# Five edits to a hybrid convolution, retention and expert layer: retention heads grouped by parity, squares written elsewhere, a projection copied by ScalarE, its gain applied in the last stage, and a turned ring of expert weights

## The chip, the cores and the metric

The kernel runs on one core of a Trainium2 chip in one launch. A core has TensorE (PE in the profile; PEld are its weight loads), VectorE (DVE), ScalarE (ACT), GpSimd (POOL) and SyncE (SP), which mainly issues DMAs. Each engine takes its own instructions strictly in order. The metric is device time in microseconds (us) from the first to the last instruction and what lies around it; runs are compared by their median.

## The reference, cut to what matters

All arrays are float32, with 1024 tokens and a width of 1024.

```python
h = rmsnorm(x, g_mix)
u, c_g, b_g, q, k, v, sg, m_c, m_r = split(h @ w_in)
y_conv = (b_g * causal_dwconv(c_g * u, conv_w)) @ w_out_conv
o = retention(rope(q), rope(k) * RET_DK**-0.5, v)    # 8 heads, key 64, value 128, chunks of 128 tokens
o = rmsnorm(o, g_ret)                                # per head
y_ret = (silu(sg) * o) @ w_out_ret
x = x + (sigmoid(m_c) * y_conv + sigmoid(m_r) * y_ret) @ w_o
x = x + hier_moe(rmsnorm(x, g_moe), ...)             # 32 experts, 2 per token, hidden width 512
ple = rmsnorm(p @ w_ple_proj, g_ple_post)            # p is 1024 x 256
x = x + sigmoid(rmsnorm(x, g_ple_in) @ w_ple_gate) * ple
out = rmsnorm(x, g_final)

# one chunk of the retention, per head:
scores = (qb @ kb.T) * decay_mask
out    = scores @ vb + (qb @ state) * q_decay
state  = state * chunk_decay + (kb * k_decay).T @ vb
```

## The kernel before, in words

A float32 matrix is split for most products into a high part (ScalarE copies it to a rounded type) and a low part (VectorE subtracts the high part from the original); three matmuls high x high, high x low, low x high make one product (`split` L187 to L189, `mm3` L192 to L195). So the program is a stream of TensorE matmuls with 512 output columns, fed by pairs of one ScalarE and one VectorE instruction.

The stages in order of time, with the profiled times:

- **Norm and q, k, v (0 to 210 us).** The tokens are taken in two halves of four tiles of 128. `norm_T` squares a tile on ScalarE with a running sum (`sumsq`, L221), VectorE makes the reciprocal root's argument and scales the tile (L235) after GpSimd's power, TensorE turns it (L240), `split` stores it in `ha` and `hb`. `qkv` multiplies by the weights `wqs`, which come in pieces of 128x1024, and copies the results `qa` out on ScalarE (L272).
- **Gate pairs with retention (210 to 520 us).** Eight gate products (`sa` to `sd`, tile `pc` of weights) carry one retention chunk each: its transposes, `scores` (L335, output `sp`), `outputs` (L349 scores x v, L353 q x state, output `op`) and the state update (L369, output `kv`) stand between the gate's matmuls. Two heads share the 128 partitions of `qt` and `kt`: the even head has partitions 0 to 63 and the odd one 64 to 127. The state is `shared` (128x1024), zeroed at the start, block-diagonal in each pair of heads.
- **Convolution, output projections, router (to 1026 us).** The router's second half ends in lists of row numbers per expert (`listed`, `ii`), by which GpSimd gathers rows from DRAM (`h2d`) into `xgb`, for three experts at first.
- **ple (1026 to 1055 us).** `p @ w_ple_proj` for 8 token tiles in two column halves: PSUM tile `pa`, squared by ScalarE with a sum into `pss` (L805, throw-away output `pj`), multiplied by the gain `g_ple_post` on VectorE (L807, output `po`) and written to DRAM (`pled`).
- **Experts (1062 to 1646 us).** Weights come by 2 MB into `raw` tiles; `prep` splits them by half tiles into the three ring tiles `hc`, `hb`, `ha` (L928 high parts, L930 low parts). The first input rows `xgb` are turned into `xp` (L949) and split into `xh` and `xl`. For the first expert half number 0 is the gate's first four k blocks, number 1 the gate's last four, 2 and 3 the same of the up projection.
- **Last stage (1646 to 1769 us).** Per token tile: the two expert rows `yb` are weighted and added (L1189), turned (`fpt`), split (`fth`, `ftl`), multiplied by the gate weights (`fo`), and the final sums and norm are made (L1205 to L1216).

Small tiles of 128x512 come from one ring of ten (`w2k`, L105); whoever takes the next one waits until the one ten tiles back is no longer read. `xssj`, `pj`, `po`, `pp` and the retention's small tiles are all of this ring. The order of instructions on each engine is made by a scheduler when the program is built; `issue_after` pins one behind another, and `high_priority` lets a block go first.

Of the kernel before, what the change touches and what calls it, by code (L numbers as in the profile page):

```python
# [75 lines left out]
def tile_kernel(ctx, tc, cst, x, p, g_mix, w_in, conv_w, g_ret, w_out_conv, w_out_ret, w_o, g_moe,  # L76
# [141 lines left out]
    def sumsq(src, name, pool=wk):  # L218
        s = pool.tile([128, 8], F32, name=name, tag="sm", bufs=4)
        j = pool.tile([128, 1024], BF, name=name + "j", tag="w2k", bufs=NW)  # L220
        A.activation(j, src, AF.Square, accum_out=s[:, 0:1])  # L221
        return s[:, 0:1]
# [72 lines left out]
    def turn(n):  # L295
        t0 = n * 128
        for b in range(2):
            pt = bank("otp", ("o", "kv")[b])
            for j in range(4):
                pe = T.transpose(pt[:, j], osb[b][:, j], ident).ins  # L300
            ot = w2k("ot").rearrange("p (a b) -> p a b", a=4)
            for j in range(4):
                A.activation(ot[:, j], pt[:, j], AF.Copy, scale=gret[:, 4 * b + j:4 * b + j + 1])
            Y.dma_start(out=od[b * 512:(b + 1) * 512, t0:t0 + 128].rearrange("(a p) t -> p a t", p=128), in_=ot)
        return pe


    def retention(n, ck):
# [20 lines left out]
        def scores(pe):  # L329
            for par in range(2):  # L330
                sp = bank("sp", ("tr", "S")[par])
                r = slice(par * 64, par * 64 + 64)
                with tc.issue_after(pe):
                    for a_ in range(4):
                        pe = T.matmul(sp[:, a_], kt[r, a_], qt[r, a_], start=True, stop=True).ins  # L335
                sb = w2k("sb").rearrange("p (a b) -> p a b", a=4)
                V.tensor_tensor(sb, sp, caus[:, None, :].to_broadcast([128, 4, 128]), op=OP.mult)
# [3 lines left out]
        def outputs(pe):  # L341
            for b in range(2):
                op = bank("op", ("o", "tr")[b])
                m_ = 0
                with tc.issue_after(pe):
                    for a_ in (2 * b, 2 * b + 1):
                        for par in range(2):
                            h = 2 * a_ + par
                            pe = T.matmul(op[:, h - 4 * b], sm[par][:, a_], v[:, h * 128:(h + 1) * 128],  # L349
                                          start=m_ == 0, stop=first, skip_group_check=True).ins  # L350
                            m_ += 1
                        if not first:
                            pe = T.matmul(op[:, (a_ % 2) * 2:(a_ % 2) * 2 + 2], qt[:, a_],  # L353
                                          state[:, a_].rearrange("p (u v) -> p u v", u=2), start=False, stop=True,
                                          skip_group_check=True).ins
# [426 lines left out]
    def ple(wpl, pin):  # L782
        gp = [pint[:, 2048:2560], pint[:, 2560:3072]]
# [11 lines left out]
        for t in range(8):  # L795
            pp = pps[t]
            for b in range(2):
# [6 lines left out]
                j = w2k("pj", BF)[:, 0:512]  # L804
                A.activation(j, a, AF.Square, accum_out=ss[:, t, b:b + 1])  # L805
                o = w2k("po")
                V.tensor_tensor(o, a, gp[b], op=OP.mult)  # L807
# [50 lines left out]
    for hf in range(2):  # L858
# [5 lines left out]
        if hf == 1:  # L864
# [4 lines left out]
            Y.dma_start(out=pint[:, 2048:3072], in_=row_bcast(g_ple_post, 1024))  # L869
# [9 lines left out]
    for e in range(3):  # L879
        gather(e)  # L880
    ple(wpl, pin)
# [35 lines left out]
    hls[1:] = hls[:0:-1]  # L917
    done = [0]

    def prep(n):  # L920
        while done[0] < min(n, 2 * len(order)):
# [5 lines left out]
            for q in (0, 1024):  # L927
                A.activation(hl[:, 0, q:q + 1024], raw[:, q:q + 1024], AF.Copy)  # L928
                with tc.issue_after(listed[0]) if 0 < h < 4 else nullcontext():
# [243 lines left out]
    gf = fw.tile([128, 1024], F32, name="gf", bufs=1)  # L1173

# [7 lines left out]
    def fin_sum(t, yb):  # L1182
# [15 lines left out]
        return th, tl, s[:, 1:2]  # L1198

# [25 lines left out]
    with tc.issue_after(last):  # L1225
        gate_load(1)
        ys.append(fin_load(1))
        fin_rows(1, ys[1])
        Y.dma_start(out=gf, in_=row_bcast(g_final, 1024))
    gate_parts(1)  # L1230
    for t in range(8):
# [3 lines left out]
        if t < 7:  # L1235
            hs.append(fin_sum(t + 1, ys[t + 1]))
        if t < 6:
# [29 lines left out]
```

## Time and profile before

| | us |
|---|---|
| Median of three runs | 1774.91 (1774.49 to 1778.44) |
| The profiled run's own time | 1771.04 |
| Its span, first to last instruction | 1769.2 |
| PE, DVE, ACT, POOL busy | 1708.2, 1265.4, 903.2, 157.2 |
| Mean granted TensorE clock | 0.990 |

A busy time sums the instructions of an engine; several engines work at once, so the times do not add up to the span. TensorE is busy nearly all the time, so what it waits for, and what it does in its busy time, is read stage by stage.

### The profile page before, as it was taken

How to read it: one execution, taken by the hardware profiler on the slowest of the kernel's cores; microseconds unless marked ns; L12 is line 12 of the kernel's file. 1: busy time of each engine (PE TensorE's matmuls, PEld its weight loads, DVE VectorE, ACT ScalarE, POOL GpSimd, SP SyncE). 2: the span in 40 equal slices, each digit the busy share in tenths (PEclk: the TensorE clock that was granted, in tenths of full speed). 3: DMA queues.
4: the chain of work that ended last, by engine and by line, in shares of the span. 5: the costliest groups of instructions: out<-in, count | busy, mean ns of one | idle time of the engine just before them, and what ended most of it. 6: DMA issues, size and time to landing. Idle time of an engine off the chain costs nothing.

```text
span 1769.2 us, 22046 instructions
## 1 busy us (share of the span) xinstructions
PE 1708.2 (97%) x8063; PEld 1325.2 (75%) x8063; DVE 1265.4 (72%) x1748; ACT 903.2 (51%) x1326; POOL 157.2 (9%) x157
## 2 busy tenths in 40 slices
PE   6999999999999999999999989999999999999697
PEld 5878788888888787788888866666666666666586
DVE  5559575666766775746455378999999988888674
ACT  4343344444222223524322257788888877778542
POOL 1000000000000000000000012222212121100010
PEclk9999999999999999999999999999999999999899
DMA  7534434444113226657556799999999999996561
GB/s 231 151 104 138 157 120 146 130 135 137 60 60 95 72 86 185 203 180 249 180 166 208 268 297 365 350 374 389 366 381 362 382 362 349 373 395 259 211 255 58
DMA packets 166401, 397.63 MB, mean 225 GB/s; under 512 B 14764, under 2 KB 85492, under 8 KB 140692
## 3 DMA queue, kind: packets, MB, share of 16 engines
q1 hardware_dynamic: 156788, 378.19, 61.3%
q0 software_dynamic: 9504, 18.02, 3.4%
q8 instruction: 64, 1.05, 0.2%
q14 instruction: 45, 0.37, 0.1%
HBM read 344.77 MB, written 57.68 MB: 227 GB/s over the span
## 4 chain that ended last, share of the span: by engine, by line
PE 74%; issue 13%; DMA 6%; DVE 4%; ACT 1%; POOL 0%; SPq 0%; POOLq 0%; DVEq 0%; ACTq 0%
PE y L193 4%; PE y L195 4%; PE y L194 4%; PE qa L193 3%; PE qa L195 3%; PE qa L194 3%; PE g L193 3%; PE g L194 3%; PE g L195 3%; PE u L194 3%; PE u L193 3%; PE u L195 3%; DMA both<-in_w_in_dram 3%; PE sd L193 2%; PE sc L193 2%
## 5 line engine op out<-in xcount | busy, mean ns | idle before, releaser
L930 DVE TENSOR_TENSOR hc<-raw,hc 128x1024 fp32r<-128x1024 f32 x128 | 154.3, 1223 | 20.4 <-ACT hc L928 19.2
L930 DVE TENSOR_TENSOR hb<-raw,hb 128x1024 fp32r<-128x1024 f32 x128 | 153.9, 1219 | 15.5 <-ACT hb L928 14.2
L930 DVE TENSOR_TENSOR ha<-raw,ha 128x1024 fp32r<-128x1024 f32 x128 | 154.1, 1222 | 13.7 <-ACT ha L928 11.7
L188 ACT ACTIVATE pc<-both 128x512 fp32r<-128x512 f32 x120 | 75.1, 629 | 157.4 <-PE sc L195 86.0
L928 ACT ACTIVATE ha<-raw 128x1024 fp32r<-128x1024 f32 x128 | 132.7, 1058 | 26.6 <-PE y L195 15.3
L928 ACT ACTIVATE hb<-raw 128x1024 fp32r<-128x1024 f32 x128 | 132.8, 1057 | 21.2 <-PE u L195 11.6
L928 ACT ACTIVATE hc<-raw 128x1024 fp32r<-128x1024 f32 x128 | 132.5, 1056 | 14.5 <-PE y L195 5.7
L189 DVE TENSOR_TENSOR pc<-both,pc 128x512 fp32r<-128x512 f32 x120 | 82.1, 686 | 27.0 <-ACT pc L188 26.6
L193 PE MATMUL y<-ph,wys 128*128 128x512 f32 x248 | 97.1, 392 | 1.9 <-ACT wys L188 1.9
L195 PE MATMUL y<-ph,wys 128*128 128x512 f32 x248 | 96.5, 390 | 0.0
L194 PE MATMUL y<-pl,wys 128*128 128x512 f32 x248 | 96.5, 389 | 0.0
L188 ACT ACTIVATE wys<-wyr 128x1024 fp32r<-128x1024 f32 x31 | 32.8, 1061 | 99.7 <-PE y L195 79.3
L193 PE MATMUL sd<-sh,pc 128*128 128x512 f32 x192 | 76.2, 397 | 3.8 <-DVE u L454 3.8
L195 PE MATMUL sd<-sh,pc 128*128 128x512 f32 x192 | 74.9, 390 | 0.0
L194 PE MATMUL sd<-sl,pc 128*128 128x512 f32 x192 | 74.8, 390 | 0.0
L189 DVE TENSOR_TENSOR wqs<-wqr,wqs 128x1024 fp32r<-128x1024 f32 x32 | 39.1, 1222 | 49.1 <-ACT wqs L188 49.1
L188 ACT ACTIVATE wqs<-wqr 128x1024 fp32r<-128x1024 f32 x32 | 33.9, 1059 | 70.2 <-PE qa L195 63.8
L769 POOL DMA_INDIRECT xgb<-h2d,ii x32 | 36.2, 1130 | 294.6 <-DVE hd L966 198.5
L188 ACT ACTIVATE pc<-bt 128x512 fp32r<-128x512 f32 x48 | 30.3, 630 | 62.7 <-PE sa L195 25.3
L558 DVE TENSOR_TENSOR msg<-y,msg 128x512 f32<-128x512 f32 x32 | 22.1, 690 | 53.7 <-PE y L195 53.7
L448 ACT ACTIVATE u<-sa 128x512 f32<-128x512 f32 x24 | 14.3, 597 | 84.1 <-PE sa L195 44.8
L193 PEld LDWEIGHTS y<-ph,wys 128*128 128x128 f32 x248 | 46.6, 188 | 12.1 <-ACT wys L188 2.8
(400 smaller groups left out, 4837.4 us busy)
## 6 DMA issues: line engine op xcount, KB each, us to landing
raw<-in_w_exp_gate_dram SPq DMA_DIRECT2D x64, 1024.0 KB, 19.7
raw<-in_w_exp_up_dram SPq DMA_DIRECT2D x64, 1024.0 KB, 17.6
raw<-in_w_exp_down_dram SPq DMA_DIRECT2D x63, 1024.0 KB, 18.8
both<-in_w_in_dram SPq DMA_DIRECT2D x24, 1024.0 KB, 5.7
wqr<-in_w_in_dram SPq DMA_DIRECT2D x32, 512.0 KB, 3.8
qd<-r SPq DMA_DIRECT2D x32, 256.0 KB, 2.4
both<-qd SPq DMA_DIRECT2D x8, 1024.0 KB, 4.8
wyr<-in_w_out_conv_dram SPq DMA_DIRECT2D x16, 512.0 KB, 3.8
```

The lines of the kernel that those rows point to most:

```text
L188: a = A.activation(hi, src, AF.Copy)
L189: V.tensor_tensor(lo, src, hi, op=OP.subtract)
L193: T.matmul(o, lh, rh, start=start, stop=False, skip_group_check=skip)
L194: T.matmul(o, lh, rl, start=False, stop=False, skip_group_check=skip)
L195: return T.matmul(o, ll, rh, start=False, stop=stop, skip_group_check=skip).ins
L448: A.activation(u2, a, AF.Copy)
L558: V.tensor_tensor(sg, y, sg, op=OP.mult)
L769: g = P.indirect_dma_start(out=xgs[e % 3], out_offset=None, in_=h2d, in_offset=bass.IndirectOffsetOnAxis(ap=ii[:, 0, e:e + 1], axis=0), bo ...
L928: A.activation(hl[:, 0, q:q + 1024], raw[:, q:q + 1024], AF.Copy)
L930: V.tensor_tensor(hl[:, 1, q:q + 1024], raw[:, q:q + 1024], hl[:, 0, q:q + 1024], op=OP.subtract)
```

## The change

1. `sumsq` writes the squares' throw-away output into the retention state `shared` and no longer into a tile of the ring of ten. The state is therefore zeroed after the second half's norm and not at the start.
2. Retention. The heads are grouped by parity: group b holds heads b, b+2, b+4, b+6, and the gain's index and the DRAM write of `turn` follow that. In `scores` the matmuls of the even and the odd heads alternate; they use rows 0 to 63 and 64 to 127 of the array and two PSUM banks. In `outputs` the four matmuls of q with a 128x256 block of state become eight of 64 rows and 128 columns that alternate in the same way, ahead of the eight of scores with v.
3. `ple` copies `pa` out by ScalarE instead of multiplying by the gain on VectorE; the squares' throw-away output goes into a spare piece of `pint`. Eight copies of one column on ScalarE take eight tiles of the ring before `ple`.
4. The gain is multiplied in the last stage on VectorE, two 128x512 products per token tile (`fin_gain`); its 512 KB are loaded there.
5. The ring of expert weights is turned: the first half goes to `hb`, the second to `ha`, the third to `hc` (before: `hc`, `hb`, `ha`). The low parts of the first half now also come behind the lists.

```diff
@@ sumsq
-        j = pool.tile([128, 1024], BF, name=name + "j", tag="w2k", bufs=NW)
-        A.activation(j, src, AF.Square, accum_out=s[:, 0:1])
+        A.activation(shared[:, 0:512].bitcast(BF), src, AF.Square, accum_out=s[:, 0:1])
@@ turn
-                A.activation(ot[:, j], pt[:, j], AF.Copy, scale=gret[:, 4 * b + j:4 * b + j + 1])
-            Y.dma_start(out=od[b * 512:(b + 1) * 512, t0:t0 + 128].rearrange("(a p) t -> p a t", p=128), in_=ot)
+                A.activation(ot[:, j], pt[:, j], AF.Copy, scale=gret[:, 2 * j + b:2 * j + b + 1])
+            Y.dma_start(out=od.rearrange("(a u p) t -> u p a t", u=2, p=128)[b, :, :, t0:t0 + 128], in_=ot)
@@ retention
         def scores(pe):
+            sp = [bank("sp", ("tr", "S")[par]) for par in range(2)]
+            for a_ in range(4):
+                for par in range(2):
+                    r = slice(par * 64, par * 64 + 64)
+                    with tc.issue_after(pe):
+                        pe = T.matmul(sp[par][:, a_], kt[r, a_], qt[r, a_], start=True, stop=True).ins
             for par in range(2):
-                sp = bank("sp", ("tr", "S")[par])
-                r = slice(par * 64, par * 64 + 64)
-                with tc.issue_after(pe):
-                    for a_ in range(4):
-                        pe = T.matmul(sp[:, a_], kt[r, a_], qt[r, a_], start=True, stop=True).ins
...
         def outputs(pe):
-            for b in range(2):
-                op = bank("op", ("o", "tr")[b])
-                m_ = 0
-                with tc.issue_after(pe):
-                    for a_ in (2 * b, 2 * b + 1):
-                        for par in range(2):
-                            h = 2 * a_ + par
-                            pe = T.matmul(op[:, h - 4 * b], sm[par][:, a_], v[:, h * 128:(h + 1) * 128],
-                                          start=m_ == 0, stop=first, skip_group_check=True).ins
-                            m_ += 1
-                        if not first:
-                            pe = T.matmul(op[:, (a_ % 2) * 2:(a_ % 2) * 2 + 2], qt[:, a_],
-                                          state[:, a_].rearrange("p (u v) -> p u v", u=2), start=False, stop=True,
-                                          skip_group_check=True).ins
+            ops = [bank("op", ("o", "tr")[b]) for b in range(2)]
+            for a_ in range(4) if not first else ():
+                for b in range(2):
+                    r = slice(b * 64, b * 64 + 64)
+                    with tc.issue_after(pe):
+                        pe = T.matmul(ops[b][:, a_], qt[r, a_], state[r, a_, b * 128:b * 128 + 128],
+                                      start=a_ == 0, stop=False, skip_group_check=True).ins
+            for b, op in enumerate(ops):
+                with tc.issue_after(pe):
+                    for a_ in range(4):
+                        h = 2 * a_ + b
+                        pe = T.matmul(op[:, a_], sm[b][:, a_], v[:, h * 128:(h + 1) * 128],
+                                      start=first and a_ == 0, stop=True, skip_group_check=True).ins
@@ ple
-                j = w2k("pj", BF)[:, 0:512]
-                A.activation(j, a, AF.Square, accum_out=ss[:, t, b:b + 1])
+                A.activation(pint[:, 3808:4064].bitcast(BF), a, AF.Square, accum_out=ss[:, t, b:b + 1])
                 o = w2k("po")
-                V.tensor_tensor(o, a, gp[b], op=OP.mult)
+                A.activation(o, a, AF.Copy)
                 Y.dma_start(out=pled[t * 128:(t + 1) * 128, cc], in_=o)
@@ before the call of ple
-            Y.dma_start(out=pint[:, 2048:3072], in_=row_bcast(g_ple_post, 1024))
+    for _ in range(8):
+        A.activation(w2k("skip")[:, 0:1], ones[:, 0:1], AF.Copy)
@@ the ring of expert weights, prep
-    hls[1:] = hls[:0:-1]
+    hls.reverse()
-                with tc.issue_after(listed[0]) if 0 < h < 4 else nullcontext():
+                with tc.issue_after(listed[0]) if h < 4 else nullcontext():
@@ last stage
+    gp = fw.tile([128, 1024], F32, name="gp", bufs=1)
+    def fin_gain(yb):
+        for c in range(2):
+            cc = slice(c * 512, (c + 1) * 512)
+            V.tensor_tensor(yb[:, 2, cc], yb[:, 2, cc], gp[:, cc], op=OP.mult)
+        Y.dma_start(out=gp, in_=row_bcast(g_ple_post, 1024))
         Y.dma_start(out=gf, in_=row_bcast(g_final, 1024))
     gate_parts(1)
+    fin_gain(ys[0])
...
             hs.append(fin_sum(t + 1, ys[t + 1]))
+            fin_gain(ys[t + 1])
```

Three places show how instructions move. The first is TensorE in the second retention chunk, between the matmuls of the gate products `sa` and `sc`; in these rows a count is of program matmuls, of which each leaves two records in the trace. Before, the first two rows stand there four times in turn, and the fourth time is followed by:

```order
L349 MATMUL op<-both,sb 128x128 x2
L353 MATMUL op<-shared,qt 128x256
L369 MATMUL kv<-both 64x128 x8
L193 MATMUL sc<-sh,pc 128x512
L194 MATMUL sc<-sl,pc 128x512
```

After, the whole of it, from the end of `sa` on:

```order
L348 MATMUL op<-shared,qt 128x128 x8
L354 MATMUL op<-both,sb 128x128 x8
L369 MATMUL kv<-both 64x128 x8
L193 MATMUL sc<-sh,pc 128x512
L194 MATMUL sc<-sl,pc 128x512
```

The four 128x256 products between pairs of `sb` products became one block of eight smaller ones ahead of all `sb` products. The second place is ScalarE at the turn from the first to the second token half, from the last copies of `qa` on. Before:

```order
L272 ACTIVATE r_775<-qa 128x512
L272 ACTIVATE r_778<-qa 128x512
L221 ACTIVATE xssj,xss<-xi 128x1024
L188 ACTIVATE wqs<-wqr 128x1024
L221 ACTIVATE xssj,xss<-xi 128x1024
L188 ACTIVATE ha<-xtq 128x4x128
L188 ACTIVATE hb<-xtp 128x4x128
L221 ACTIVATE xssj,xss<-xi 128x1024
```

After (its two first squares of the second half stand some 20 rows earlier, at the end of the first half's norm):

```order
L271 ACTIVATE r_771<-qa 128x512
L271 ACTIVATE r_774<-qa 128x512
L188 ACTIVATE ha<-xtq 128x4x128
L188 ACTIVATE hb<-xtp 128x4x128
L220 ACTIVATE shared,xss<-xi 128x1024
L188 ACTIVATE ha<-xtq 128x4x128
L188 ACTIVATE wqs<-wqr 128x1024
L188 ACTIVATE hb<-xtp 128x4x128
```

The split of the second half's first tile follows the last copy of `qa` at once. The third place is ScalarE at the end of `ple`, where the first expert starts. Before:

```order
L805 ACTIVATE pj,pss<-pa 128x512 x5
L928 ACTIVATE hc<-raw 128x1024 x2
L188 ACTIVATE xh<-xp 128x352 x2
L928 ACTIVATE hc<-raw 128x1024 x2
L928 ACTIVATE hb<-raw 128x1024 x2
```

After:

```order
L803 ACTIVATE pin,pss<-pa 128x512
L805 ACTIVATE po<-pa 128x512
L188 ACTIVATE xh<-xp 128x352 x2
L928 ACTIVATE hb<-raw 128x1024
L928 ACTIVATE hc<-raw 128x1024 x2
L928 ACTIVATE hb<-raw 128x1024
L928 ACTIVATE ha<-raw 128x1024 x2
```

The first expert's input split `xh` now comes before the high parts in `hc`, not behind them.

## Rows read from the trace of the kernel before

**Rows 1.** The page's part 1: busy time, share of the span and instructions by engine.
```profile
PE 1708.2 (97%) x8063; PEld 1325.2 (75%) x8063; DVE 1265.4 (72%) x1748; ACT 903.2 (51%) x1326; POOL 157.2 (9%) x157
```

**Rows 2.** Windows: from:to and length, busy time by engine, clock, DMA share, GB/s.
```profile
110.00:120.00 10.00, 7.76 (x34) 5.71 (x35) 7.41 (x14) 6.69 (x13) 1.65 (x3) 0.83 0.41 133
190.00:520.00 330.00, 327.32 (x1700) 271.35 (x1699) 213.01 (x345) 128.09 (x257) 18.09 (x19) 0.99 0.37 118
...
1660.00:1700.00 40.00, 39.08 (x174) 31.22 (x174) 31.80 (x55) 21.84 (x41) 3.85 (x7) 0.96 0.77 297
```

**Rows 3.** TensorE's groups by line and shape, 190 to 520 us: records, busy us, mean ns.
```profile
L335 PE MATMUL sp<-qt,kt 64*128 64x128 f32 x128 | 13.7, 285 | 0.0
```

**Rows 4.** TensorE's timeline, one retention chunk: start, length, what, records, idle before.
```profile
242.00 0.39 PE L195 MATMUL sd<-sh,pc 128*128 128x512 f32 x1
242.32 1.71 PE L335 MATMUL sp<-qt,kt 64*128 64x128 f32 x16
243.96 0.50 PE L193 MATMUL sa<-ha,pc 128*128 128x512 f32 x1
...
246.82 0.61 PE L349 MATMUL op<-both,sb 128*128 128x128 f32 x4
247.27 0.60 PE L353 MATMUL op<-shared,qt 128*128 128x256 f32 x2
...
250.43 1.09 PE L369 MATMUL kv<-both 128*64 128x128 f32 x16
251.45 0.50 PE L193 MATMUL sc<-sh,pc 128*128 128x512 f32 x1
```

**Rows 5.** The same timeline, 243.0 to 243.4 us alone.
```profile
242.75 0.83 PE L335 MATMUL sp<-qt,kt 64*128 64x128 f32 x9
```

**Rows 6.** TensorE's timeline where the second token half begins.
```profile
112.14 0.63 PE L240 MATMUL xtq<-cs,xi 128*128 128x128 f32 x4 [3.44 <-issue]
...
113.46 0.80 PE L193 MATMUL qa<-wqs,ha 128*128 128x512 f32 x1
...
116.73 0.40 PE L194 MATMUL qa<-wqs,ha 128*128 128x512 f32 x1
116.96 0.39 PE L195 MATMUL qa<-wqs,ha 128*128 128x512 f32 x1
```

**Rows 7.** ScalarE's timeline at the same place.
```profile
109.23 1.05 ACT L221 ACTIVATE xssj<-xi 128x1024 bf16<-128x1024 f32 x1
```

**Rows 8.** ScalarE's timeline near the start.
```profile
24.19 1.06 ACT L188 ACTIVATE wqs<-wqr 128x1024 fp32r<-128x1024 f32 x1 [2.05 <-DMA wqr<-in_w_in_dram]
```

**Rows 9.** ScalarE's timeline, end of ple.
```profile
1058.35 0.60 ACT L805 ACTIVATE pj<-pa 128x512 bf16<-128x512 f32 x1 [4.59 <-DMA pled<-po]
...
1059.79 2.00 ACT L928 ACTIVATE hc<-raw 128x1024 fp32r<-128x1024 f32 x2 [0.76 <-DVE po L807]
1061.70 0.80 ACT L188 ACTIVATE xh<-xp 128x352 fp32r<-128x352 f32 x2
```

**Rows 10.** TensorE's timeline where the experts begin.
```profile
1062.20 0.73 PE L193 MATMUL g<-hc,xh 128*88 128x512 f32 x1 [6.99 <-ACT xh L188]
...
1065.54 0.40 PE L193 MATMUL g<-hc,xh 128*88 128x512 f32 x1
```

**Rows 11.** GpSimd's timeline, the first gather.
```profile
1043.16 1.18 POOL L769 DMA_INDIRECT xgb<-h2d,ii  x1 [16.62 <-DMA pled<-po]
```

**Rows 12.** TensorE's timeline, start of ple.
```profile
1028.50 0.50 PE L193 MATMUL pa<-wpl,pp 128*128 128x512 f32 x1 [1.24 <-ACT pp L188]
```

**Rows 13.** ScalarE's timeline before ple.
```profile
1024.96 1.99 ACT L928 ACTIVATE ha<-raw 128x1024 fp32r<-128x1024 f32 x2
...
1028.08 0.37 ACT L188 ACTIVATE pp<-ptp 128x256 fp32r<-128x256 f32 x1
```

**Rows 14.** VectorE's groups by line and shape, last stage.
```profile
L1207 DVE TENSOR_TENSOR yb<-yb,sg 128x512 f32<-128x512 f32 x16 | 11.0, 687 | 0.2
```

**Rows 15.** ScalarE's waits in the expert stage, 1070 to 1600 us: total, times, longest.
```profile
ACT hb L928 <- DMA raw<-in_w_exp_up_dram: 0.6, 2, 0.3
```

More of the change, by code (lines that the diff above doesn't have):

```diff
@@ L329, in scores @@
         def scores(pe):
-            for par in range(2):
-                sp = bank("sp", ("tr", "S")[par])
-                r = slice(par * 64, par * 64 + 64)
-                with tc.issue_after(pe):
-                    for a_ in range(4):
-                        pe = T.matmul(sp[:, a_], kt[r, a_], qt[r, a_], start=True, stop=True).ins
+            sp = [bank("sp", ("tr", "S")[par]) for par in range(2)]
[4 more added lines that the diff above has]
+                        pe = T.matmul(sp[par][:, a_], kt[r, a_], qt[r, a_], start=True, stop=True).ins
+            for par in range(2):
                 sb = w2k("sb").rearrange("p (a b) -> p a b", a=4)
-                V.tensor_tensor(sb, sp, caus[:, None, :].to_broadcast([128, 4, 128]), op=OP.mult)
+                V.tensor_tensor(sb, sp[par], caus[:, None, :].to_broadcast([128, 4, 128]), op=OP.mult)
                 sm.append(sb)
@@ L782, in ple @@
     def ple(wpl, pin):
-        gp = [pint[:, 2048:2560], pint[:, 2560:3072]]
         ss = wk.tile([128, 8, 2], F32, name="pss", bufs=1)
```

## The prediction, made before the changed kernel ran

> **What bounds the kernel now.** I read the busy times first: TensorE is busy 1708 of 1769.2 us, so at most 61 us are waits and the rest must come from matmuls that get shorter or fewer [rows 1]. Then the windows, to see where it is not simply full [rows 2]. In the retention stage it is busy 327.32 of 330 us, so there only cheaper matmuls help; at 110 to 120 us it is busy 7.76 of 10 at a granted clock of 0.83; in the last stage it is nearly full while VectorE is busy 31.80 of 40. Last the timelines at the three holes that the edits touch: 3.44 us ahead of the second half's transposes [rows 6], 6.99 us ahead of the first expert [rows 10], 1.24 us at the start of ple [rows 12].
>
> **Retention, edit 2.** One chunk shows the present price. The scores take from 242.32 to 243.96, 1.64 us for 16 records; the outputs from 246.82 to 250.43, 3.61 us [rows 4]. Of these the products with v are 16 records at (247.27 - 246.82) / 4 = 0.113 us, 1.80 in all, so the state's part is 1.81.
> What alternating row halves cost is not in the trace as such, but two rows come near. In the scores before, the even heads' records all precede the odd heads'. The narrow window over that border has 9 records in 0.83 us; one is 0.285 long [rows 3], so 8 steps take 0.545, or 0.068 each [rows 5]. That is far under 0.113: the odd heads began while the even ones still ran. And the state update, which alternates column halves, needs 1.02 us for 16 records (250.43 to 251.45). I take 0.068: 16 x 0.068 = 1.09 us.
> Scores: 1.64 - 1.09 = 0.55, times 8 chunks, 4.4 us saved. State part: 1.81 - 1.09 = 0.72, less an added change of mode, because this block used to run on all 128 rows. The change into the scores starts 0.32 us behind the matmul before it (242.00 to 242.32), where full-width neighbours follow after 0.23 (116.73 to 116.96, [rows 6]); the way back shows in the first wide matmul's 0.50 against 0.39. I estimate 0.25 for both: 0.47 saved in each of the 7 chunks that have a state, 3.3 us. Together 7.7 us. Bounds: with no overlap the scores gain nothing and the state loses 7 x 0.25 = 1.7; with perfect overlap, 0.056 per record, 0.74 x 8 + 0.66 x 7 = 10.5.
> The Trainium skill, "TensorEngine Tiling (Array Packing)", Key Properties, says both that different tiles run in parallel and that a change of mode drains TensorE. The first agrees with the 0.068; by the second each chunk pays one drain more, which the 0.25 stands for. Were a drain 0.7 us, the state part would gain nothing, this edit would be worth 4.4 us, and the sum below 3.3 less.
>
> **Second half's norm, edit 1.** TensorE waits 3.44 us until 112.14, though the last product before it is done, because ScalarE makes the squares (109.23) only behind the four copies of qa, and the scaling hangs on them [rows 6, 7]. The squares needed a tile of the ring of ten; now they need none. In the new order the first two stand at the end of the first half's norm, where ScalarE idles 2.05 us for a weight DMA [rows 8]: two squares of 1.05 fill that hole nearly exactly, so I put nothing on the start (at most 1 us). So the transposes can follow at 108.70 (112.14 - 3.44); ScalarE's split of ha comes at once behind the last copy, at 109.23, takes some 0.6, and the first product can start near 109.85 instead of 113.46: 3.6 us. Also the seven products from 113.46 to 116.73 take 3.27 us at the low clock against 7 x 0.23 = 1.61; with a hole well under 1 us I expect most of that 1.66 back. On the other side, the third tile's square now stands behind the first tile's split, so its transposes may wait some 0.6, and the state's zeroing moves onto a busy VectorE. I take 4.0 (2 to 5).
>
> **From ple to the first expert, edits 3 and 5.** TensorE's last transposes end at 1062.20 - 6.99 = 1055.21. What holds it is a queue on ScalarE: the last square waits 4.59 us for a tile of the ring that a DMA to pled still reads, then come two high parts of hc (2.00 us), then xh [rows 9]. After the change the squares take no ring tile, so ple draws 1.5 tiles per column half instead of 2.5 and the tile that a copy reuses is some 7 halves old instead of 4 to 5; and xh stands directly behind the last copy. With a square of 0.60, a copy of as much, and 0.5 from xh's start to the first product (1061.70 to 1062.20, [rows 9, 10]), all behind the last pa at about 1054.3, TensorE restarts at some 1056: a hole of 0.8. For a write that lands late I take 1.5, so 5.5 us are saved. The seven listed products from 1062.20 to 1065.54 take 3.34 us for 1.61; after the 1.24 us hole the first product takes 0.50 against 0.73 here [rows 10, 12], so I count 1.0 of this 1.7 back. Together 6.5 (2 to 8). ScalarE now does a square with its sum and a copy per column half, some 1.2 us by these lengths, and a split of pp (0.37, [rows 13]) per token tile, 2.8 in all, against TensorE's 12 products at 0.23 and two transposes, about 3.0: it keeps up, with little to spare. VectorE loses the gain's products ahead of the lists, so the first gather (1043.16, [rows 11]) comes no later.
>
> **The eight skipped tiles.** They stand on ScalarE ahead of ha's first part, where it now starts at 1024.96, and wait for the DMAs that still read the router's tiles. TensorE waits there for pp, which ScalarE does at 1028.08 [rows 12, 13]. I estimate 1.2 us later (0.5 to 2), all of it on the path.
>
> **Last stage, edit 4.** 16 products of 0.687 us, 11 us on VectorE [rows 14]. Per token tile, which takes TensorE 48 products of 0.23 and some transposes, about 12 us, that is 1.37 us more: VectorE's 31.80 of 40 becomes about 36 [rows 2], still under TensorE's 39.08. The cover is thin at the stage's start, where the new load stands ahead of g_final's and the first gain ahead of the first gate's sum; I take 1.0 us lost (0 to 4).
>
> **The sum.** -7.7 - 4.0 - 6.5 + 1.2 + 1.0 = -16.0 us. From the profiled run's own 1771.04 that gives 1755.0; from the median 1774.91, which is 3.87 above, 1758.9. I predict 1757.
>
> **Rivals.**
> *The row halves don't overlap.* Then retention gives +1.7 instead of -7.7: 1757 + 9.4 = 1766. The 0.068 speaks against it; that it was measured at one border, where the first stream was ending, leaves room. 0.12.
> *Another wait takes the place of ScalarE's at the first expert.* The writes to pled share the DMA engines with weights and gathers, and the first expert's third half (hc) is split later than before: if TensorE stands some 6 us there or at the norm all the same, 1763. Weights as the limit of the whole expert stage, so that an early start is given back, speaks little: ScalarE waits 0.6 us for them in 530 us [rows 15]. 0.18.
> *VectorE paces the last stage.* Its idle time there is in-order waiting, so the 11 us and a first wait of 3 might all show: 1757 - 1 + 14 = 1770. TensorE's lead over each tile's sums speaks against. 0.06.
> *Slower: alternating halves run worse than a single stream.* If a record in the other half could not start before the one ahead has ended, each would take its 0.285 [rows 3]: 16 x 0.285 = 4.56 us, 2.92 more per scores and 2.75 more per state block, 8 x 2.92 + 7 x 2.75 = 43 us, and 1757 + 7.7 + 43 = 1808. It turns the sign when the 240 records lose the other edits' 8.3 us, at 0.035 each, a step of about 0.148. The border in rows 5 speaks against it. 0.05.
> *The edits do nothing:* the norm's and ple's holes are set elsewhere and the overlap is small: 1771. 0.04.
>
> **How the numbers follow.** The forecast has 0.55, with a range of its own from 1750 to 1763. 0.2%, 3.5 us, is what a measurement of this kernel can tell, so faster means under 1771.4. The forecast, the first two rivals and part of the third lie there: 0.83. Within: the rest of the third, the last and tails of the others, 0.10. Slower: the fourth, and a sum of small losses, 0.07. The range 1747 to 1769 takes in the first two rivals and the best ends of the larger terms.
>
> **What the profile after would show.** Right: 16 score records in about 1.1 us and outputs in about 3.1; the first product of the second half within 1.5 us of the last of the first, at full clock; a hole under 2 us ahead of the first expert with the wait not on a DMA; a hole at ple's start of 2 to 3 us; the last stage as long as before to 2 us. Wrong: score records at 0.11 or more; ScalarE still waiting for pled; TensorE waiting for VectorE in the last stage.

## The result and the profile after

| | us | ratio to before, 95% interval |
|---|---|---|
| Before, median of four runs beside it | 1775.68 | |
| Changed, median of four runs | 1753.52 (1750.26 to 1755.26) | 0.9871 [0.9851, 0.9890] |
| Changed, in a second comparison | 1756.09 | 0.9892 [0.9875, 0.9908] |
| Changed, in a third comparison | 1757.65 | 0.9900 [0.9883, 0.9916] |
| Profiled span, before and after | 1769.2 and 1748.4 | |

The change makes the kernel 18 to 22 us faster. Forecast were 1757 us and a sum of 16.0.

The profile after is that of the fastest of the four runs (1750.26), and of the study's fourteen traces it is the only one whose granted TensorE clock stays at 1.00 from 25 us to the end of the experts. Two more traces of the same kernel, a1 and a2 below, have spans of 1755.0 and 1751.1 us: held against them the table's sum would be -14.2 and -18.2 instead of -20.8. In the table, read a difference of 1 to 2 us with that in mind.

The first view is where the time went, stage by stage. The starts of TensorE's first and last instructions of each stage were read from both timelines; a row is the length of a stretch.

| stretch of TensorE's timeline | before | after | change | forecast |
|---|---|---|---|---|
| start to the first half's last product | 108.31 | 109.18 | +0.87 | 0 |
| from there to the second half's first product | 5.15 | 1.57 | -3.58 | -3.6 |
| from there to the end of q, k, v | 92.77 | 92.16 | -0.61 | -0.4 |
| from there to the first retention transposes | 6.61 | 5.05 | -1.56 | none |
| to the last retention output's transposes | 214.21 | 206.62 | -7.59 | -7.7 |
| from there to ple's first product | 601.45 | 601.78 | +0.33 | +1.2 |
| ple | 25.69 | 25.54 | -0.15 | 0 |
| xp's transposes and the hole behind them | 8.01 | 1.83 | -6.18 | -5.5 |
| first expert's first product to its first y | 26.77 | 25.67 | -1.10 | -1.0 |
| experts | 557.10 | 556.67 | -0.43 | 0 |
| to the last stage's first product | 14.35 | 14.24 | -0.11 | 0 |
| last stage's products | 98.16 | 97.43 | -0.73 | +1.0 |

The page's part 1 of the changed kernel answers to [rows 1]: TensorE is busy 11.6 us less and waits some 9 us less.

```profile
PE 1696.6 (97%) x8119; PEld 1317.8 (75%) x8119; DVE 1264.4 (72%) x1748; ACT 909.2 (52%) x1350; POOL 161.5 (9%) x157
```

The same retention chunk as in [rows 4], in TensorE's timeline of the changed kernel:

```profile
236.54 0.39 PE L195 MATMUL sd<-sh,pc 128*128 128x512 f32 x1
236.86 1.16 PE L334 MATMUL sp<-qt,kt 64*128 64x128 f32 x16
237.95 0.50 PE L193 MATMUL sa<-ha,pc 128*128 128x512 f32 x1
...
240.90 1.16 PE L348 MATMUL op<-shared,qt 64*128 64x128 f32 x16
241.99 2.05 PE L354 MATMUL op<-both,sb 128*128 128x128 f32 x16
243.97 1.09 PE L369 MATMUL kv<-both 128*64 128x128 f32 x16
```

Scores take 1.09 us (236.86 to 237.95), the number that the forecast took from the border between the heads. The same timeline, 237.3 to 237.5 us alone, answers to [rows 5]:

```profile
237.07 0.61 PE L334 MATMUL sp<-qt,kt 64*128 64x128 f32 x8
```

These are four pairs, one record of each row half, that start 0.007 us apart in the trace. A record lasts 0.27, so the other 0.34 are the three steps between the pairs: 0.11 a pair, 0.056 a record. That is the forecast's bound for perfect overlap; the rest of the 1.09, some 0.2 us, lies at the block's two ends.

Outputs take 3.07 (240.90 to 243.97) instead of 3.61, 0.54 less where 0.47 was forecast. The change of mode is seen too: 16 products with v, 1.80 us by themselves, take 1.98 (241.99 to 243.97) behind the 64-row block.

The entry of the second half, TensorE, answers to [rows 6]:

```profile
109.42 0.60 PE L239 MATMUL xtq<-cs,xi 128*128 128x128 f32 x4
109.85 0.60 PE L239 MATMUL xtp<-cs,xi 128*128 128x128 f32 x4
110.75 0.50 PE L193 MATMUL qa<-wqs,ha 128*128 128x512 f32 x1 [0.30 <-ACT ha L188]
...
114.54 0.66 PE L239 MATMUL xtq<-cs,xi 128*128 128x128 f32 x4 [0.34 <-DVE ha L189]
```

The 3.44 us hole is 0.30, a small one of 0.34 is new at the third tile as forecast, and the first product's 0.50 (0.80 before) says that the clock did not fall. The window agrees, against [rows 2]: in 110 to 120 us the granted clock is 1.00 and no longer 0.83.

```profile
110.00:120.00 10.00, 9.36 (x50) 7.23 (x48) 8.14 (x14) 6.43 (x12) 1.10 (x2) 1.00 0.49 166
```

At the first expert, against [rows 10], TensorE's hole is 0.82 us instead of 6.99:

```profile
1041.90 1.01 PE L949 MATMUL xp<-cs,xgb 88*128 88x88 f32 x8
1043.73 0.46 PE L193 MATMUL g<-hb,xh 128*88 128x512 f32 x1 [0.82 <-ACT xh L188]
1044.03 0.40 PE L194 MATMUL g<-hb,xh 128*88 128x512 f32 x1
1044.78 0.47 PE L195 MATMUL g<-hb,xl 128*88 128x512 f32 x1 [0.35 <-DVE xl L189]
```

ScalarE's timeline, against [rows 9, 13], shows why, and that the eight skipped tiles waited for nothing: they take 0.84 us in one piece, and pp still starts 1.7 us behind TensorE's transposes of `ptp` (1014.23 to 1015.94; before, 1026.36 to 1028.08), since the second high part of ha now stands behind it.

```profile
1012.82 0.84 ACT L880 ACTIVATE skip<-cs 128x1 f32<-128x1 f32 x8
...
1015.94 0.36 ACT L188 ACTIVATE pp<-ptp 128x256 fp32r<-128x256 f32 x1
...
1042.15 0.60 ACT L803 ACTIVATE pin<-pa 128x512 bf16<-128x512 f32 x1 [0.21 <-PE pa L195]
...
1042.74 0.59 ACT L805 ACTIVATE po<-pa 128x512 f32<-128x512 f32 x1
1043.22 0.82 ACT L188 ACTIVATE xh<-xp 128x352 fp32r<-128x352 f32 x2
```

But the last row of TensorE's group above has a wait that the trace of before does not have: L195 waits 0.35 us for xl. It is small here, and the experiments are mostly about it.

### The profile page after: what moved, and what is told of

Its sections match the earlier page's. It is cut to its first block, busy times and chain, and to the rows that moved or that the text cites. A ratio compares the mean times of both kernels' runs of the same rounds, so it can differ in the third digit from the quotient of the medians.

```text
span 1748.4 us, 22161 instructions
## 1 busy us (share of the span) xinstructions
PE 1696.6 (97%) x8119; PEld 1317.8 (75%) x8119; DVE 1264.4 (72%) x1748; ACT 909.2 (52%) x1350; POOL 161.5 (9%) x157
## 4 chain that ended last, share of the span: by engine, by line
PE 71%; issue 13%; DMA 6%; DVE 6%; ACT 2%; POOL 0%; SPq 0%; POOLq 0%; DVEq 0%; ACTq 0%
PE y L195 4%; PE y L193 4%; PE y L194 4%; PE g L195 3%; PE u L194 3%; PE g L194 3%; PE g L193 3%; PE u L193 3%; PE u L195 3%; DMA both<-in_w_in_dram 3%; PE qa L194 2%; PE qa L195 2%; PE qa L193 2%; PE sd L193 2%; PE sc L193 2%
## 5 line engine op out<-in xcount | busy, mean ns | idle before, releaser
L195 PE MATMUL y<-ph,wys 128*128 128x512 f32 x248 | 96.8, 391 | 0.1
L195 PE MATMUL sd<-sh,pc 128*128 128x512 f32 x192 | 75.0, 391 | 0.0
L188 ACT ACTIVATE pc<-bt 128x512 fp32r<-128x512 f32 x48 | 30.3, 630 | 66.0 <-PE sa L195 25.0
```

The source lines that it names most:

```text
L188: a = A.activation(hi, src, AF.Copy)
L195: return T.matmul(o, ll, rh, start=False, stop=stop, skip_group_check=skip).ins
```

## The experiments

The theory of the prediction: concurrent row halves, the norm's hole and the queue on ScalarE each give what the trace of before says, independently. The first rival was that the neighbours of an edit and not the edit itself bring its share.

**e1, retention undone.** `turn`, `scores` and `outputs` as before, all else changed.

```diff
-            sp = [bank("sp", ("tr", "S")[par]) for par in range(2)]
+            for par in range(2):
+                sp = bank("sp", ("tr", "S")[par])
...
```

Expected: 

> The changed kernel with the retention written as before, all else changed. Theory (row halves overlap): the stretch from the first retention transposes to the last one's output grows by 7.6 us (201.4 - 193.8 in the two profiles' terms: 214.2 before, 206.6 after), the time by 7 to 8 us, to about 1761. Rival (the retention's gain comes from the neighbours, e.g. less waiting around it): under 3 us of it comes back. The holes at the second half's norm (0.3 us) and at the first expert (0.8 us) stay as in the changed kernel by both.

Measured: 1774.05 us, ratio 0.9992 [0.9982, 1.0002]: the whole gain was gone. Neither number had been expected. The retention stretch itself grew by 7.7 us (206.62 to 214.29), as the theory says. From the first expert's first product to its first y 11.8 more were lost (37.44 against 25.67), where TensorE waits for xl, and VectorE for a write to pled; and the hole ahead of that did not stay as expected, it is 2.67 instead of 0.82 us. TensorE's and VectorE's timelines of e1:

```profile
1058.72 0.46 PE L193 MATMUL g<-hb,xh 128*88 128x512 f32 x1 [2.67 <-ACT xh L188]
...
1070.13 0.73 PE L195 MATMUL g<-hb,xl 128*88 128x512 f32 x1 [10.72 <-DVE xl L189]
```

```profile
1069.55 0.95 DVE L189 TENSOR_TENSOR xl<-xp,xh 128x352 fp32r<-128x352 f32 x2 [11.33 <-DMA pled<-po]
```

xl is a tile of the experts' pool, which takes the space that ple's pool leaves. By the addresses in the built programs (xl has 2816 bytes a partition at 207424, ring tiles of 2048 begin at 206048, 208096 and 210144) it lies over three ring tiles, and waits until the last po written from any of them has landed. Which po these are depends on how the ring of ten stands when ple ends, and that on every ring tile taken before, in the retention too. In the changed kernel they are the 9th to 11th of 16 po at the latest, in e1 the 16th, the very last. In the kernel before it was the 13th, and the 6.99 us hole hid it: xl waited for no write there.

Some traces also have the time at which such a write landed, and it is the newest po under xl that VectorE waits for: in the changed kernel's first trace the 11th landed at 1044.08 us and xl starts at 1044.20, in e7 the 15th at 1050.29 and xl at 1050.37, in e1b the 12th at 1053.60 and xl at 1053.72. In e2 the 10th had landed at 1048.29, and xl starts at 1050.16 without a wait.

**e5, one row half after the other.** The order of the two loops in scores and in the state products exchanged:

```diff
-            for a_ in range(4):
-                for par in range(2):
+            for par in range(2):
+                for a_ in range(4):
```

Expected: 

> The changed kernel, but in scores and in the state products the eight matmuls of the even heads all come before those of the odd heads, not in turn. Theory (the two row halves stream at the same time when neighbours alternate): 16 records take 1.64 us again instead of 1.09, in 8 scores and 7 state blocks, 15 x 0.55 = 8.2 us slower than the changed kernel, about 1762, so a little slower in this stage than before. Rival (64-row, 128-column blocks are cheaper in themselves, the order does not matter): 1.09 stays and the time too, 1753 to 1754.

Measured: 1764.12 us, ratio 0.9933 [0.9916, 0.9949], 8.0 above the changed kernel measured beside it (1756.09). TensorE's timeline of e5, the second chunk, has both blocks at 1.64 us (242.79 to 244.43):

```profile
238.19 1.71 PE L334 MATMUL sp<-qt,kt 64*128 64x128 f32 x16
...
242.79 1.71 PE L348 MATMUL op<-shared,qt 64*128 64x128 f32 x16
244.43 2.05 PE L354 MATMUL op<-both,sb 128*128 128x128 f32 x16
```

Eight matmuls, four of one row half and then four of the other, in place of the same eight in turn: it is the alternation that pays, as the theory has it. The ring and the 11th po under xl are unchanged here.

**e6, one excursion per chunk.** The eight state products directly behind the scores; the second output bank and the state update's bank exchanged.

```diff
+            ops.extend(bank("op", ("o", "kv")[b]) for b in range(2))
+            for a_ in range(4) if not first else ():
+                for b in range(2):
+                    ...
-            kvs.append(bank("kv", "kv"))
+            kvs.append(bank("kv", "tr"))
```

Expected: 

> The changed kernel, with the state products directly behind the scores, so that each chunk goes into the 64-row mode once and not twice (the outputs' second bank and the state update's bank are swapped for that). In the changed kernel a change of mode shows as 0.32 instead of 0.23 us ahead of the block and 1.98 instead of 1.80 us in the 16 products behind it. Theory (a change costs these 0.27 us): 7 x 0.27 = 1.9 us faster than the changed kernel. Rival (a change drains TensorE for longer, up to 0.7): 5 us. Second rival (the swapped banks are not free in time): TensorE waits ahead of the state products, slower by up to 1 us a chunk, 7 in all.

Measured: 1757.60 us, ratio 0.9896 [0.9880, 0.9913], not faster than the changed kernel (1756.09). TensorE's timeline of e6:

```profile
236.86 1.16 PE L334 MATMUL sp<-qt,kt 64*128 64x128 f32 x16
237.86 1.06 PE L340 MATMUL op<-shared,qt 64*128 64x128 f32 x16
...
241.71 1.95 PE L354 MATMUL op<-both,sb 128*128 128x128 f32 x16
243.58 1.09 PE L369 MATMUL kv<-both 128*64 128x128 f32 x16
...
1047.74 0.73 PE L195 MATMUL g<-hb,xl 128*88 128x512 f32 x1 [3.69 <-DVE xl L189]
```

The retention stretch is 204.31 us, 2.3 less than in the changed kernel, 0.33 for each of the seven chunks with a state. The rows show most of it where a change of mode went: scores take 1.00 (236.86 to 237.86) instead of 1.09, products with v 1.87 (241.71 to 243.58) instead of 1.98. So a change there and back costs a little more than the 0.27 expected. It was lost again at xl, under which the newest po is now the 15th: 3.69 us, and low clock behind it (0.73 against 0.47 in the changed kernel).

**a1, a2, the changed kernel again.** Expected: 

> The changed kernel once more beside the others on the same chip: 1750 to 1756 us, and as a second trace: if the full clock behind the 1.5 us hole at 204 us (low in the trace of before) is a matter of this kernel, it is full here too; if it falls by chance, it may be low.

And: 

> The changed kernel beside e10 on one chip, in five rounds: 1752 to 1757 us. In the two traces so far the wait of TensorE for xl was 0.4 and 1.6 us and the stretch from the first expert's first product to its first y 25.7 and 28.4 us; a third trace shows again how far it varies.

Measured: 1756.09 and 1757.65 us, both just above what was expected. TensorE's wait for xl was 1.55 and 0.60 us, against 0.35 in the first trace. The clock behind the hole at 204 us, which nothing in the change touches, fell in one and not in the other. TensorE's timeline there, before, then the changed kernel's first trace, then a1:

```profile
207.76 0.50 PE L193 MATMUL sb<-sh,pc 128*128 128x512 f32 x1 [1.53 <-ACT pc L188]
...
212.84 1.04 PE L319 MATMUL qkp<-cs,both 128*128 128x128 f32 x8
```

```profile
204.44 0.50 PE L193 MATMUL sb<-sh,pc 128*128 128x512 f32 x1 [1.53 <-ACT pc L188]
...
207.96 1.04 PE L318 MATMUL qkp<-cs,both 128*128 128x128 f32 x8
```

```profile
204.08 0.50 PE L193 MATMUL sb<-sh,pc 128*128 128x512 f32 x1 [1.53 <-ACT pc L188]
...
209.13 1.03 PE L318 MATMUL qkp<-cs,both 128*128 128x128 f32 x8
```

From the hole's end to the transposes it is 5.08, 3.52 and 5.05 us for the same work. The granted clock is 0.50 (the lower level, 1.2 GHz) in before from 209 to 211 us and in a1 from 205.5 to 207.5, and 1.00 in the changed kernel's first trace from 205.5 to 207.5. So the 1.56 us in the table is no part of the change; of the 14 traces of this study 5 have the low clock there. The start of ple is such a place too: its stretch is 25.2 to 25.7 us in the 7 traces with the full clock and 26.5 to 27.2 in the 7 with the low clock behind the hole there (a1: 27.04; the changed kernel's other two: 25.54 and 25.55).

**e1b, e1 with two skipped tiles instead of eight.**

```diff
-    for _ in range(8):
+    for _ in range(2):
         A.activation(w2k("skip")[:, 0:1], ones[:, 0:1], AF.Copy)
```

Expected: 

> The kernel of e1_ret_back with 2 copies of one column instead of 8 ahead of ple. e1 lost 20 us where 7.6 were due; its trace has VectorE waiting 11.3 us ahead of the first expert's xl for a write to pled, and in the built program xl lies over ring tiles of which the last was written out by the 16th and last po (in the changed kernel: by the 11th at the latest). With 2 copies it is the 12th. Theory (xl waits until the newest write from under it has landed, and the retention only changed which tiles lie there): the wait falls from 11.3 to 2 to 4 us, the time to 1761 to 1764. Rival (the retention itself delays what follows): 1774 again.

Measured: 1770.68 us, ratio 0.9979 [0.9968, 0.9990]. The wait for xl fell from 10.7 to 2.4 us as expected; the time fell by less. The built program's order differs at the first expert as well: in e1, as in the changed kernel, hc's high parts come behind the first of hb, here behind those of hb and ha, and TensorE waits for them. TensorE's waits in e1b:

```profile
PE u L193 <- ACT hc L927: 3.2, 1, 3.2
PE g L195 <- DVE xl L189: 2.4, 1, 2.4
```

So the alignment sets the wait for xl, 8.3 us of it here, but the time gives back only 3.4 (2.3 by the ratios to before): from the first product to the first y e1b still takes 35.64 us (e1 37.44, the changed kernel 25.67 to 28.41), part of it the wait for hc and low clock. How much of e1's loss is due to the alignment alone is not shown. The retention alone is the 7.6 to 7.7 us in the stretches of the traces of before, e1 and e1b.

**e7, no skipped tiles.** The two lines of the diff above removed. Expected: 

> The changed kernel without the eight one-column copies. Theory: they cost nothing (0.84 us on ScalarE, none on TensorE) but set which ring tiles lie under xl; without them the newest is the 15th po, and TensorE waits some 6 to 9 us for xl, 1760 to 1764. Rival (the copies are only a cost on ScalarE ahead of the second pp): 0 to 1 us faster than the changed kernel.

Measured: 1758.28 us, ratio 0.9910 [0.9894, 0.9927]. VectorE's and TensorE's timelines:

```profile
1050.37 0.96 DVE L189 TENSOR_TENSOR xl<-xp,xh 128x352 fp32r<-128x352 f32 x2 [3.67 <-DMA pled<-po]
```

```profile
1050.95 0.73 PE L195 MATMUL g<-hb,xl 128*88 128x512 f32 x1 [3.07 <-DVE xl L189]
```

The wait is there (15th po), at half the size that was expected. From the first product to the first y it is 31.2 us against 25.7, 27.4 and 28.4 in the changed kernel's three traces. The time was expected to be 1760 to 1764; held against the changed kernel's three medians, none of them measured beside it, e7 is 1 to 5 us slower.

**e2, squares in ring tiles again.**

```diff
-        A.activation(shared[:, 0:512].bitcast(BF), src, AF.Square, accum_out=s[:, 0:1])
+        j = pool.tile([128, 1024], BF, name=name + "j", tag="w2k", bufs=NW)
+        A.activation(j, src, AF.Square, accum_out=s[:, 0:1])
```

Expected: 

> The changed kernel with the squares' throw-away output in ring tiles again (under xl the newest is then the 10th po, so no loss there). Theory: the 3.4 us hole ahead of the second half's transposes comes back, with low clock behind it, 4 to 5 us slower than the changed kernel, about 1759. On the 1.5 us hole at 204 us: if the low clock behind it hangs on what went before in the kernel, it is low again here as in before; it was full in both traces of the changed kernel... if it is full here, it is not tied to the first hole.

Measured: 1756.92 us, ratio 0.9907 [0.9892, 0.9924]. The hole is back on TensorE:

```profile
112.72 0.63 PE L240 MATMUL xtq<-cs,xi 128*128 128x128 f32 x4 [3.43 <-issue]
```

Up to the end of q, k, v it is 3.9 us behind the changed kernel's first trace. xl waits for no write here (10th po): first product to first y takes 25.17 us, which gives some of it back (25.67, 28.41 and 27.42 in the changed kernel). So the medians do not show the edit's worth; the trace does. The clock at 204 us is low, but as a1 has that too it tells nothing of the first hole.

**e4, the ring of weights as before.**

```diff
-    hls.reverse()
+    hls[1:] = hls[:0:-1]
```

(and `0 < h < 4` again). Expected: 

> The changed kernel with the ring of expert weights as before (first half to hc, second to ha, third to hb), the same ring tiles under xl. Theory: ScalarE then makes both high parts of hc behind xh, 2.0 us, and VectorE the low parts, 2.4, before the first expert's products can run; the hole of 0.8 us ahead of the first expert grows to 2 to 4 us, with low clock behind it: 3 to 5 us slower than the changed kernel. Rival (the copy on ScalarE alone closed the hole, the ring's order is worth nothing): within 1 us of it.

Measured: 1755.42 us, ratio 0.9892 [0.9874, 0.9911], against 1757.65 for the changed kernel beside it: no loss in time. The hole grew as the theory said, and the first product is at low clock, but xl, which comes behind the high parts then, waits for no DMA any more:

```profile
1045.62 0.73 PE L193 MATMUL g<-hc,xh 128*88 128x512 f32 x1 [2.71 <-ACT xh L188]
```

The turned ring takes 1.9 us of ScalarE's work away from ahead of xh. From xp's transposes to the first y e4 takes 30.6 us, the changed kernel 27.5, 30.3 and 29.3 in its three traces: where xl waits longest for pled (a1, 1.55 us) nearly the whole gain is gone again, and the times show none.

**e8, the gain twice.** Each product by the gain in the last stage is made two times, so the output carries it once too often.

```diff
+            for _ in range(2):
+                V.tensor_tensor(yb[:, 2, cc], yb[:, 2, cc], gp[:, cc], op=OP.mult)
```

Expected: 

> The changed kernel with every product by the gain in the last stage made twice (the result is scaled by the gain once more): 16 more VectorE products of 0.69 us, 11 us. Theory (TensorE covers them): the last stage, 99.8 us from the first transposes to the last product, grows by 0 to 2 us. Rival (VectorE paces the stage): by 8 to 11 us.

Measured: 1755.94 us, ratio 0.9884 [0.9868, 0.9901]. From the first to the end of the last gate product it takes 97.47 us, against 97.43 with the gain once and 98.16 before. VectorE's group in e8, and the window 1680 to 1700 us:

```profile
L1205 DVE TENSOR_TENSOR yb<-yb,gp 128x512 f32<-128x512 f32 x32 | 21.0, 685 | 0.0
```

```profile
1680.00:1700.00 20.00, 19.93 (x93) 15.95 (x92) 19.11 (x35) 7.85 (x17) 3.23 (x4) 1.00 0.60 218
```

VectorE is busy 19.11 of 20 us, and TensorE still 19.93: even the 21 us of these products, which the last stage of before did not have, cost nothing.

**e10, a version that takes the wait away.** e6 with xl as two tiles of four k blocks each, and every tile of an expert's input in a place of its own, so that the first half of xl lies under no ring tile:

```diff
-        xh = mw.tile([128, 8, CAP], F32R, name="xh", tag="xh", bufs=2)
-        xl = mw.tile([128, 8, CAP], F32R, name="xl", tag="xl", bufs=2)
+        xh = mw.tile([128, 8, CAP], F32R, name="xh", tag=f"xh{e % 2}", bufs=1)
+        xl = [mw.tile([128, 4, CAP], F32R, name="xl", tag=f"xl{g}{e % 2}", bufs=1) for g in range(2)]
...
```

Expected at first: 

> e6_one_excursion (state products behind the scores) with xl as two tiles of four k blocks each, the first of which lies under no ring tile of ple, the second under the 12th po. Theory: e6 kept its 2.3 us in the retention but lost 3.8 us and low clock at xl, which waited for the 15th po; without that wait the first expert starts as in the best run of the changed kernel, and the time is 1748 to 1753 in every run. Rival (the wait moves on to xl's second half or the low parts behind it): 1755 to 1757.

And in five rounds beside the changed kernel: 

> e10_low_apart beside the changed kernel on one chip, in five rounds. Theory: 2.3 us from the single excursion, and 0 to 3 us from the wait at xl that it does not have: 2 to 5 us under the changed kernel of the same call. Rival (both gains are inside the spread): within 1 us of it.

Measured: 1752.71, ratio 0.9879 [0.9863, 0.9896]; then 1751.83, ratio 0.9857 [0.9841, 0.9874], where the changed kernel had 1757.65 and 0.9900 [0.9883, 0.9916] on the same chip: 5.8 us less by the medians, more than the 2 to 5 expected, and the intervals do not meet. VectorE's timeline shows the two halves, TensorE's that the first product with xl waits for nothing:

```profile
1043.15 0.53 DVE L189 TENSOR_TENSOR xl<-xp,xh 128x352 fp32r<-128x352 f32 x1 [0.47 <-ACT xh L188]
1045.24 0.53 DVE L189 TENSOR_TENSOR xl<-xp,xh 128x352 fp32r<-128x352 f32 x1 [1.57 <-DMA pled<-po]
```

```profile
1043.73 0.46 PE L195 MATMUL g<-hb,xl 128*88 128x512 f32 x1
```

The second half still waits 1.57 us for pled, but it is not needed before the thirteenth product. First product to first y takes 25.2 us in both of its traces.

That the wait is gone is shown; how much time that is worth is not. The first comparison's 0.9879 lies between the changed kernel's 0.9871 and 0.9900. The two runs profiled side by side took 1753.18 us (e10) and 1752.92 (a2): e10 gains 2.3 us in the retention and 2.2 at the first expert, and loses 1.4 by the clock at the 204 us hole and 2.8 in the experts, which take 558.0 and 559.6 us in its traces against 556.7 to 556.8 in the changed kernel's three. In the longer of the two TensorE waits for late splits of weights near their end (0.9 us for hb's high part); why they come late was not settled.

The newest po under xl (by the addresses) and TensorE's wait at its first product with xl (by the traces):

| | newest of 16 po under xl | wait, us |
|---|---|---|
| e10 | none under the first half | 0 |
| e2 | 10th | 0 |
| changed, three traces | 11th | 0.4, 1.6, 0.6 |
| e5, e8 | 11th | 1.8, 1.5 |
| e4, where VectorE comes 2.4 us later | 11th | 0 |
| e1b | 12th | 2.4 |
| e7, e6 | 15th | 3.1, 3.7 |
| e1 | 16th | 10.7 |

## Why the prediction was right, and where it was not

- **Retention, -7.7.** Right in mechanism and size: -7.59 in the table, scores 1.09 us as taken, and e5 shows that the alternation is the cause. That 0.068 a record came out to the digit is in part luck: at the border in [rows 5] some steps overlapped and some did not, while the alternating block is 0.056 a record with 0.2 us at its ends. The added change of mode was put at 0.25 us; e6 gives 0.33 for one change there and back. The 0.7 us at which the state products would have gained nothing was not met. The Trainium skill, "TensorEngine Tiling (Array Packing)", Key Properties, says that such a change drains TensorE. The trace agrees in sign: 1.98 us instead of 1.80 for the products with v behind a 64-row block.
- **Norm, -4.0.** The hole went as forecast (-3.58, clock back up). What failed is "I put nothing on the start": 0.87 us were lost there. Of these 0.33 are spread: the first product starts at 18.00 us before and at 18.33 after, and between 18.0 and 19.8 in the fourteen traces. The other 0.54 are the edit's: from the first product to the half's last it is 90.31 us before, 90.29 in e2, which undoes the edit, and 90.81 to 90.85 in the changed kernel's three traces.
- **ple to the first expert, -6.5.** -7.28 with the clock (-6.18 and -1.10) in the first trace, -4.5 and -5.5 in a1 and a2. The hole came out at 0.82 where 0.8 had been worked out and 1.5 taken. That the queue on ScalarE was the cause is read from the two traces: no square waits for pled any more. Only the ring's part of it was undone (e4, 1.9 us of the 6.2); the copy's part has no run of its own. The step missed a wait on the other side. It looked for late pled writes at ScalarE, where a copy reuses a ring tile, and not at the next pool, whose tiles lie in the same space. "Another wait takes the place of ScalarE's at the first expert" was a rival with 0.18, and this is its mechanism; in the changed kernel it costs 0.4 to 1.6 us, in a1 and a2 low clock behind it as well, and only with another alignment the 6 us of the rival or more (e1).
- **Skipped tiles, +1.2.** Wrong: TensorE's hole ahead of ple is 1.23 us, 1.24 before, and the 2 to 3 us named as a sign did not come. ScalarE waited for no DMA at these tiles, and the order behind them gave pp's place back. Their cost was asked for, and not what they do: by e7 they set the ring so that an early po lies under xl.
- **Last stage, +1.0.** Wrong in sign, -0.73 (-0.3 to -1.7 with the three traces). The cover is far thicker than "thin at the start": e8 hides twice the products. VectorE's idle time was in-order waiting for ScalarE's sigmoid, which the products partly fill: 16.5 us in 11 waits before, 10.0 in 7 after.
- **The sum.** -16.0 against -20.8 in the profiles: by the table 0.9 and 1.7 from the last two points, 1.6 from the clock at 204 us, which is chance, 0.8 from ple to the first expert, and small stretches of either sign. The comparisons gave -22.2 and twice some -18, the traces -20.8, -14.2 and -18.2. In the three traces it is the clock at that hole, near 735 us and at ple's start, and the wait and the clock at xl, that differ most. That the forecast of 1757 lies within 1 us of the later medians (1756.09 and 1757.65) is partly luck: two costs of 2.2 us in all did not come, and of the 6.5 us at the first expert 1 to 2 did not come in those traces either.

## What to carry to other kernels

Where one pool's tiles take over another's space, the first tiles of the new stage can wait for the last DMAs that read the old ones; look up what lies under the tile that is needed first, and give it a place that nothing late has used. An experiment that undoes one part can move such an overlap and so measure that instead of the part: hold the stretches of the two traces against each other before the totals. Matmuls of 64 rows should alternate between the two halves and stand together, so that the array changes its mode once.

## What the runs showed of the hardware that was not expected

Eight 64-row matmuls (16 records), four in one row half and then four in the other, take 1.64 us, the same eight in turn 1.09 (e5 and the changed kernel); the state update, whose matmuls take the two column halves in turn, had 1.02 already [rows 4]. The granted clock after one and the same 1.53 us hole of TensorE fell in 5 of 14 traces and stayed full in 9, in different runs of one kernel too; after the 3.4 us holes it fell in each of the two traces that have them. The low clock cost 1.5 us at the former hole (5.05 against 3.52 us for the same work in the changed kernel).
